# The last scan of a hybrid backbone with its gate units and weight splits in another order, and two query rotations of Mixer B in later steps

## The chip, the cores and the metric

The kernel runs on one core of a Trainium2 chip. The metric is device time in microseconds (us); lower is better. A kernel is timed in several executions, of which the median counts. One execution more is recorded by the profiler: its span runs from the first instruction to the last, and its own time is that of the whole launch. Below, TensorE is the matmul engine (PE in rows; PEld is its weight load), VectorE is DVE, ScalarE is ACT, GpSimd is POOL and SyncE is SP.

## The reference

The model is a block of four layers over 256 latent and 256 context tokens with 1024 features, in float32. The layers' mixers are A, B, C, A. Each layer has a mixer and an MLP, each behind an RMS norm with shift, scale and gate from a conditioning vector.

- Mixer A is a bidirectional mLSTM in chunks of 128 tokens with 8 heads: `h = num / max(|den|, exp(-m))` for each direction, the two directions added, then for each head `h * rsqrt(mean(h*h) + eps) * head_g`, and `(sigmoid(o) * h) @ w_out`, where `o` is 1024 columns of the projection `x @ w_in`. In the last layer only the latent tokens have an output.
- Mixer B is attention with 16 query heads and 4 key heads of 64 features. Latent queries and keys are turned by a 2-D rotary embedding; context ones are not. Scores go through a softmax with a learned sink for each head.

## The kernel before

All matrix products of weights are done as three float32r products: a weight tile of 128x1024 is loaded (`w_dma`, on SP's queue), cast to a high part on ScalarE (`w_hi`, line 242), and the low part is the difference, on VectorE (`w_lo`, line 247), which then issues the load of the tile four places on. `w_half` does the cast at once and returns the difference as a function to be called later; `w_get(0)` takes the next tile and splits it only if that was not done. There are 4 raw tiles and 5 pairs of parts. A unit is 128 output columns: 8 chunks of 3 matmuls (lines 392 to 394), and half a unit is 4 chunks.

The order on every engine is the order of the code; nothing is rescheduled. Waits are set by a tracker: two instructions on different engines wait for each other where they touch the same data, or the same of the eight PSUM banks.

**The last scan** (`scan`, with `last` true) goes over four head pairs, pr = 0 to 3. The output gate's 8 units (m = 0 to 7) are worked in between, in halves, by the generator `fillers`: every `next(fill)` issues half a unit into bank 4 (even m in its first 256 columns, odd m in the others). The sigmoid of a unit has three steps. The exponential (line 975, ScalarE) is issued with the unit's second half; the clamp on VectorE with Ln and Exp on ScalarE (lines 977 to 979) with the next unit's first half; the two combining operations on VectorE (lines 981 and 982) where `settle` is called. In an iteration stand:

- `states(pr)`: products of keys and values into columns 0 to 448 of banks 6 and 7 (line 1062), then six VectorE operations that read them (lines 1071 and 1073);
- a half unit; `mask` (VectorE, line 948) and `weights` (ScalarE, line 956) for the next pair; `outputs` (lines 1087 and 1096, banks 0 to 3);
- `out(pr - 1, hh)`: two transposes (line 1148) into columns 256 to 511 of bank 7 or 6, and line 1150 on VectorE that reads them and multiplies the gate;
- `keys` (line 1034, bank 5), `scores` (line 1026, columns 0 to 255 of banks 6 and 7), `keys_weigh` (line 1044) and `weigh` (line 1052, which reads the scores);
- the second half of the unit; `finish` (denominators on VectorE, then lines 1115 and 1117); `head_squares` (ScalarE); another unit's two halves; `head_norm` (three ScalarE and three VectorE operations on 128x4, then line 1140 on ScalarE).

Before the change the second unit's first half comes ahead of `head_norm` and its second half after it, each behind one `w_half`.

**Mixer B** projects ten units of queries and keys. `rotate` copies a unit's latent half to SBUF (line 1325), and its returned function `rest` does the rotation: a matmul with a permutation (line 1329), three VectorE operations (lines 1331 to 1333), and `put`: two copies on ScalarE (line 1317) and two subtractions on VectorE (line 1319). The functions wait in the list `pend`. The attention goes in steps y, two head pairs each: scores of the pairs 2y and 2y+1 (`s1`), their maxima on VectorE, exponentials on ScalarE, normalisation (`normalise(y - 1)`), transposes of the probabilities (`turn`) and, two steps on, value products (`pv`, line 1467). Pairs alternate between banks 3, 4 and banks 6, 7 for their scores. The unit 8 is projected ahead of step 1, the unit 9 at the end of step 1 in bank 2. Bank 2 is next used by the value products of step 5. The rotated queries of units 8 and 9 are first read in step 9.

Of the kernel before, what the change touches and what calls it, by code (L numbers as in the profile page):

```python
# [208 lines left out]
class Body:  # L209
# [748 lines left out]
    def scan(self, l, i, last, sp, lp, dnm, dar, qT, kT, vx, tok, saved, n):  # L958
# [6 lines left out]
        bk = self.banks  # L965
# [19 lines left out]
        def fillers():  # L985
            late = None
            for m in range(8):
                w = self.w_get(0)
                o = bk[4][:, m % 2 * T : m % 2 * T + T] if last else bk[4]
                self.unit(o, w, self.x_chunk, full, range(4))  # L990
                if late:
                    next(late)
                yield
                self.unit(o, w, self.x_chunk, full, range(4, NK))
                cur["late"] = late
                late = cur["last"] = sigmoid(m, o)
                next(late)
                yield
# [15 lines left out]
        def mask(pr, d):  # L1014
            self.scan_mask(pr, d)

        def weights(pr, d):
            self.scan_exp(pr, d, tok, outc)
# [11 lines left out]
        def keys(pr):  # L1030

            kt = bk[5].rearrange("p (c k) -> p c k", c=4)
            for tcn in range(4):
                nc.tensor.transpose(kt[:, tcn, :], kT[:, pr, tcn * 128 : tcn * 128 + 128], self.ident)
# [14 lines left out]
        def weigh(pr, d):  # L1049
            for hh in range(2):  # L1050
                e = cur["D", pr, d, hh]
                nc.vector.tensor_tensor(out=e, in0=e, in1=bk[6 + hh][:, :n], op=ALU.mult)
# [25 lines left out]
        def outputs(pr, sid):  # L1078


            def place(d, hh, c):
                return bk[2 * d + hh][:, (c % 2) * 256 : (c % 2) * 256 + 129]

            for d in range(2):
                for hh in range(2):
                    for c in (2 * sid, 2 * sid + 1):
                        nc.tensor.matmul(  # L1087
                            place(d, hh, c), lhsT=cur["D", pr, d, hh][:, c * 128 : c * 128 + 128], rhs=vx[:, c, 2 * pr + hh, :],
                            start=(c == 2 * sid), stop=False, skip_group_check=True,
                        )  # L1090
            for pos in (1,) if sid else (2, 3):
                for d in range(2):
                    c = ORDERS[d][pos]
                    for hh in range(2):
                        b = 64 * hh
                        nc.tensor.matmul(
                            place(d, hh, c), lhsT=cur["qa", pr, d][b : b + 64, c * 128 : c * 128 + 128],
                            rhs=cur["C", pr, d, pos - 1][b : b + 64, :], start=False, stop=True, skip_group_check=True,
                        )
# [44 lines left out]
        def out(pr, hh, tp=bk[5]):  # L1144
            h = 2 * pr + hh
            for c in range(nch):
                t_ = slice(c * 128, c * 128 + 128)
                nc.tensor.transpose(tp[:, t_], cur["h", pr, hh][:, t_], self.ident)
            hg = self.hgn[:, i * 8 + h : i * 8 + h + 1]
            nc.vector.scalar_tensor_tensor(  # L1150
                out=sg[:, h, :n], in0=tp[:, :n], scalar=hg, in1=sg[:, h, :n], op0=ALU.mult, op1=ALU.mult
            )

        fill = fillers()
# [7 lines left out]
        for d in range(2):  # L1162
            weigh(0, d)
        low = self.w_half()
        next(fill)
        for pr in range(4):
            more = pr < 3
            for hh in range(2):
                cur["h", pr, hh] = sp.tile([128, n], F32, tag="hacc", name="hacc", bufs=4)
            if more and not last:  # L1170
                self.scan_load(lp, pr + 1, dnm, dar, n, last)
            if more:
                self.scan_qa(lp, pr + 1, qT, n)
            if pr < 2 and last:
                self.scan_load(lp, pr + 2, dnm, dar, n, last)
            states(pr)
            if not last:
                outputs(pr, 1)
            if pr and not last:
                head_norm(pr - 1)  # L1180
            next(fill)
            if last:

                if pr:
                    out(pr - 1, 0, bk[7][:, 256:512])
                if more:
                    for d in range(2):
                        mask(pr + 1, d)
                        weights(pr + 1, d)
                outputs(pr, 0)  # L1190
                if more:
                    keys(pr + 1)
                    scores(pr + 1)
                    keys_weigh(pr + 1)
                    weigh(pr + 1, 0)
                    weigh(pr + 1, 1)
                next(fill)
                if not more:
                    split(0)
                    split(1)  # L1200
                finish(pr, 0)
                if pr:
                    out(pr - 1, 1, bk[6][:, 256:512])
                settle()
                low()
                if more:
                    head_squares(pr)
                    low = self.w_half()
                    next(fill)
                    head_norm(pr)  # L1210
                    low()
                    low = self.w_half()
                    next(fill)
                    settle()
                continue
            finish(pr, 1)
            if pr:
                out(pr - 1, 0)
            if more:
                mask(pr + 1, 0)  # L1220
            low()
            next(fill)
            if more:
                weights(pr + 1, 0)
                low = self.w_half()
            if pr:
                out(pr - 1, 1, bk[6])
            if more:
                mask(pr + 1, 1)
            settle()  # L1230
            if more:
                keys(pr + 1)
                weights(pr + 1, 1)
                next(fill)
                scores(pr + 1)
                keys_weigh(pr + 1)
            else:
                split(0)
                split(1)
            outputs(pr, 0)  # L1240
            if more:
                weigh(pr + 1, 0)
                weigh(pr + 1, 1)
                low()
                low = self.w_half()
                finish(pr, 0)
                head_squares(pr)
                next(fill)
                settle()
# [35 lines left out]
    def mixer_b(self, l, i):  # L1285
        nc, tc = self.nc, self.tc
        with ExitStack() as st:
# [5 lines left out]
            pend = []  # L1293
# [70 lines left out]
            bk = self.banks  # L1364
# [123 lines left out]
            def query(u, o, between, ahead):  # L1488
                w = self.w_get(ahead)
                self.unit(o, w, self.x_chunk, ALL, range(4))  # L1490
                between()
                self.unit(o, w, self.x_chunk, ALL, range(4, NK))
                evac(u, o, ALL)
# [17 lines left out]
            for y in range(1, N + 3):  # L1511
                more = y < N
                late = block_end(y - 4) if y >= 5 and y % 2 == 1 else None
                t = 2 * (y - 2)
                turns = 2 <= y < N + 2
                if more:
                    s1(2 * y)
                    maxima(2 * y)
                if y >= 3:
                    pv(y - 3)  # L1520
                if turns:
                    turn(t)
                if y == 2:
                    pend.pop(0)(bk[5])
                if y in (N, N + 1):
                    begin(bk[3 + 3 * (y - N)])
                if more:
                    exps(2 * y)
                    s1(2 * y + 1)
                    maxima(2 * y + 1)  # L1530
                if turns:
                    turn(t + 1)
                if late:
                    late()
                if more:
                    exps(2 * y + 1)
                if y <= N:
                    normalise(y - 1)
                if y in (N, N + 1):
                    begin(bk[4 + 3 * (y - N)])  # L1540
                if y == 1:
                    query(9, bk[2], lambda: pend.pop(0)(bk[5]), 0)
                if N - 3 <= y <= N + 1:
                    self.wsplit_to(self.wsplit + 1)
                if y > N:
                    c = slice(4 * (y - N - 1), 4 * (y - N - 1) + 4)
                    nc.gpsimd.dma_start(out=self.h[:, c, :], in_=saved[:, c, :])
# [336 lines left out]
```

## Time and profile before

| | us |
|---|---|
| time, median of 3 executions | 2101.82 |
| lowest, highest | 2101.45, 2102.55 |
| the profiled execution: its own time | 2103.67 |
| its span | 2101.8 |

| engine | share of the span busy |
|---|---|
| TensorE | 97% |
| TensorE weight load | 82% |
| VectorE | 70% |
| ScalarE | 45% |
| GpSimd | 4% |

A busy TensorE is one that has matmuls under way; it may still run at the lower of its two clocks. The granted clock of a stretch is 1.00 for 2.4 GHz and 0.50 for 1.2 GHz, and a mean of both in between. The last scan lies at about 1802 to 1886 us of the span, the attention of Mixer B at about 686 to 800.

### The profile page before, as it was taken

What the parts mean: (1) busy time and instruction counts of PE and PEld (TensorE: products, weight loads), DVE (VectorE), ACT (ScalarE), POOL (GpSimd) and SP (SyncE); (2) the same over time, 40 slices, a digit from 0 to 9 for tenths busy, and PEclk for the clock granted to TensorE, in tenths of its full rate; (3) what the DMA queues carried; (4) which work ended last, traced back from release to release, by engine and by line L of the source; (5) the groups of instructions that cost most, each with busy time, mean ns of one, the idle gap of its engine ahead of it and who ended that gap; (6) DMA issues with size and microseconds to landing.
All of it is one profiled execution on the core that took longest, in us unless ns stands there. A gap on an engine that the chain in (4) does not pass through costs nothing.

```text
span 2101.8 us, 29107 instructions
## 1 busy us (share of the span) xinstructions
PE 2038.5 (97%) x11154; PEld 1724.8 (82%) x11154; DVE 1472.1 (70%) x2600; ACT 943.6 (45%) x1778; POOL 81.5 (4%) x136
## 2 busy tenths in 40 slices
PE   6999999999999999999999999999999999979998
PEld 3778898888888768888888988888888898878997
DVE  5558768778778785777777754577777764567665
ACT  3437662423336674523324432362332445456554
POOL 0133000000000000000000000000000001200000
PEclk9999999999999999999999999999999999989999
DMA  9873437666653004455566233245656525436663
GB/s 298 276 232 111 136 96 207 188 194 198 186 154 130 2 26 146 143 179 190 183 189 190 81 120 99 81 148 178 188 185 189 175 87 158 115 95 191 184 187 92
DMA packets 96732, 326.03 MB, mean 155 GB/s; under 512 B 17728, under 2 KB 18896, under 8 KB 95696
## 3 DMA queue, kind: packets, MB, share of 16 engines
q1 hardware_dynamic: 81184, 293.81, 44.9%
q0 software_dynamic: 14864, 29.83, 4.7%
q8 instruction: 87, 1.43, 0.3%
q10 hardware_dynamic: 544, 0.52, 0.1%
q14 instruction: 53, 0.43, 0.1%
HBM read 319.73 MB, written 4.33 MB: 154 GB/s over the span
## 4 chain that ended last, share of the span: by engine, by line
PE 58%; DVE 2%; ACT 1%; issue 0%; DVEq 0%; ACTq 0%
PE bank L392 16%; PE bank L393 15%; PE bank L394 15%; PE bank L409 3%; PE bank L410 1%; PE bank L626 1%; PE bank L629 1%; PE bank L627 1%; PE bank L442 1%; PE bank L444 1%; PE bank L443 1%; PE bank L1087 0%; DVE wlo L247 0%; ACT whi L242 0%; DVE hacc L1117 0%
## 5 line engine op out<-in xcount | busy, mean ns | idle before, releaser
L392 PE MATMUL bank<-x,whi 128*128 128x512 f32 (+1 forms) x1568 | 570.5, 364 | 16.7 <-ACT h L975 13.9
L242 ACT CAST whi<-raw 128x1024 fp32r<-128x1024 f32 x374 | 388.0, 1046 | 416.9 <-PE bank L393 347.0
L247 DVE TENSOR_TENSOR wlo<-raw,whi 128x1024 fp32r<-128x1024 f32 x374 | 456.2, 1227 | 159.1 <-ACT whi L242 158.7
L393 PE MATMUL bank<-x,whi 128*128 128x512 f32 (+1 forms) x1568 | 564.9, 360 | 0.7 <-DVE x L1008 0.6
L394 PE MATMUL bank<-x,wlo 128*128 128x512 f32 (+1 forms) x1568 | 564.9, 360 | 0.0
L354 DVE SCALAR_TENSOR_TENSOR junk<-ada,cbc 128x1024 bf16<-128x1024 f32 x320 | 390.6, 1221 | 10.0 <-DMA ada<-in_ada 5.6
L392 PEld LDWEIGHTS bank<-x,whi 128*128 128x128 f32 x1568 | 298.9, 191 | 66.5 <-ACT h L975 16.3
L393 PEld LDWEIGHTS bank<-x,whi 128*128 128x128 f32 x1568 | 299.1, 191 | 44.1 <-DVE x L1008 1.2
L394 PEld LDWEIGHTS bank<-x,wlo 128*128 128x128 f32 x1568 | 299.0, 191 | 43.8
L392 PE MATMUL bank<-hh,whi 128*128 128x512 f32 (+1 forms) x872 | 321.1, 368 | 0.0
L393 PE MATMUL bank<-hh,whi 128*128 128x512 f32 (+1 forms) x872 | 320.5, 368 | 0.0
L394 PE MATMUL bank<-hh,wlo 128*128 128x512 f32 (+1 forms) x872 | 320.5, 368 | 0.0
L712 DVE TENSOR_TENSOR hh<-q,hh 128x512 fp32r<-128x512 f32 (+1 forms) x137 | 81.5, 595 | 161.7 <-ACT q L711 161.3
L709 ACT ACTIVATE r<-bank 128x512 f32<-128x512 f32 (+1 forms) x137 | 71.0, 518 | 267.0 <-PE bank L394 265.6
L392 PEld LDWEIGHTS bank<-hh,whi 128*128 128x128 f32 x872 | 164.4, 188 | 27.7
L393 PEld LDWEIGHTS bank<-hh,whi 128*128 128x128 f32 x872 | 164.4, 188 | 27.3
L394 PEld LDWEIGHTS bank<-hh,wlo 128*128 128x128 f32 x872 | 164.4, 188 | 27.0
L585 DVE SCALAR_TENSOR_TENSOR h<-bank,mod,h 128x256 f32<-128x256 f32 x248 | 110.1, 479 | 100.6 <-PE bank L394 100.6
L479 ACT ACTIVATE sq<-h 128x256 f32<-128x256 f32 (+1 forms) x74 | 36.2, 489 | 134.6 <-DVE h L585 114.2
L626 PE MATMUL bank<-x,whi 128*128 128x256 f32 x312 | 80.5, 287 | 3.5 <-ACT x L547 3.5
L409 PE MATMUL bank<-hh,whi 128*128 128x512 f32 x224 | 79.3, 399 | 0.0
L627 PE MATMUL bank<-x,wlo 128*128 128x256 f32 x312 | 79.3, 283 | 0.0
(281 smaller groups left out, 2381.3 us busy)
## 6 DMA issues: line engine op xcount, KB each, us to landing
raw<-in_wts SPq DMA_DIRECT2D x374, 512.0 KB, 4.0
ada<-in_ada SPq DMA_DIRECT2D x160, 512.0 KB, 3.7
start<-in_ada SPq DMA_DIRECT2D x16, 512.0 KB, 8.9
first<-in_ada POOLq DMA_DIRECT2D x12, 512.0 KB, 6.0
cbc<-line POOLq DMA_DIRECT2D x4, 1024.0 KB, 7.6
rb<-dnm POOLq DMA_DIRECT2D x16, 256.0 KB, 6.8
ab<-dar POOLq DMA_DIRECT2D x16, 256.0 KB, 10.0
h<-in_hin SPq DMA_DIRECT2D x4, 512.0 KB, 8.1
```

Of the source, the lines that this page charges most:

```text
L242: self.nc.scalar.copy(hi, self.raw[j])
L247: self.nc.vector.tensor_tensor(out=lo, in0=self.raw.pop(j), in1=hi.bitcast(F32), op=ALU.subtract)
L354: nc.vector.scalar_tensor_tensor(out=junk, in0=w, scalar=1.0, in1=self.cbc[:, s, :], op0=ALU.mult, op1=ALU.mult, accum_out=self.mods[l][:, ...
L392: mm(out, lhsT=whi, rhs=xhi, start=first, stop=False)
L393: mm(out, lhsT=whi, rhs=xlo, start=False, stop=False)
L394: mm(out, lhsT=wlo, rhs=xhi, start=False, stop=last)
L409: mm(o, lhsT=w[0][:, c], rhs=x2[:, :, LT], start=(k == 0), stop=(k == NK - 1))
L585: self.nc.vector.scalar_tensor_tensor(out=self.h[:, m, a:b], in0=o[:, a - sl.start : b - sl.start], scalar=mod[:, gate + m, s : s + 1], in ...
L626: mm(o[:, :T], lhsT=w[0][:, c], rhs=hi[:, sl], start=(k == 0), stop=False)
L627: mm(o[:, :T], lhsT=w[1][:, c], rhs=hi[:, sl], start=False, stop=False)
L709: nc.scalar.activation(r[:, :n], o, AF.Relu)
L712: nc.vector.tensor_tensor(out=hl[:, sl], in0=q[:, :n], in1=hh[:, sl].bitcast(F32), op=ALU.subtract)
```

## The change

In the last scan, both halves of the second unit are issued together, ahead of `head_norm`, so that the unit's exponential stands ahead of the norm in ScalarE's queue. The two casts of an iteration come together after `head_norm`, and their differences (`low`) are called in the next iteration: one ahead of `mask`, one behind `weights`. `out(pr - 1, 0)` moves from ahead of `mask` to behind `outputs`. In Mixer B the rotation of unit 8 moves from the middle of unit 9's projection to the end of step 2, the rotation of unit 9 from the middle of step 2 to the end of step 3, and both use bank 2 for the permutation, not bank 5.

```diff
--- before.py
+++ after.py
@@ -1162,6 +1162,7 @@
         for d in range(2):
             weigh(0, d)
         low = self.w_half()
+        lows = [low]
         next(fill)
         for pr in range(4):
             more = pr < 3
@@ -1181,13 +1182,16 @@
             next(fill)
             if last:
 
-                if pr:
-                    out(pr - 1, 0, bk[7][:, 256:512])
+                lows.pop(0)()
                 if more:
                     for d in range(2):
                         mask(pr + 1, d)
                         weights(pr + 1, d)
+                if lows:
+                    lows.pop(0)()
                 outputs(pr, 0)
+                if pr:
+                    out(pr - 1, 0, bk[7][:, 256:512])
                 if more:
                     keys(pr + 1)
                     scores(pr + 1)
@@ -1202,15 +1206,12 @@
                 if pr:
                     out(pr - 1, 1, bk[6][:, 256:512])
                 settle()
-                low()
                 if more:
                     head_squares(pr)
-                    low = self.w_half()
+                    next(fill)
                     next(fill)
                     head_norm(pr)
-                    low()
-                    low = self.w_half()
-                    next(fill)
+                    lows = [self.w_half(), self.w_half()]
                     settle()
                 continue
             finish(pr, 1)
@@ -1520,8 +1521,6 @@
                     pv(y - 3)
                 if turns:
                     turn(t)
-                if y == 2:
-                    pend.pop(0)(bk[5])
                 if y in (N, N + 1):
                     begin(bk[3 + 3 * (y - N)])
                 if more:
@@ -1539,7 +1538,9 @@
                 if y in (N, N + 1):
                     begin(bk[4 + 3 * (y - N)])
                 if y == 1:
-                    query(9, bk[2], lambda: pend.pop(0)(bk[5]), 0)
+                    query(9, bk[2], lambda: None, 0)
+                if y in (2, 3):
+                    pend.pop(0)(bk[2])
                 if N - 3 <= y <= N + 1:
                     self.wsplit_to(self.wsplit + 1)
                 if y > N:
```

## Rows read from the trace of the kernel before

**Rows 1.** The page's first part: busy time and share of the span, by engine.

```profile
PE 2038.5 (97%) x11154; PEld 1724.8 (82%) x11154; DVE 1472.1 (70%) x2600; ACT 943.6 (45%) x1778; POOL 81.5 (4%) x136
```

**Rows 2.** TensorE's waits, 1800 to 1900 us: waiter, releaser, us in total, times, longest.

```profile
PE bank L392 <- ACT h L975: 13.7, 4, 4.5
```

**Rows 3.** Timeline of TensorE, last scan: start, us, line, operation [idle before].

```profile
1815.15 0.39 PE L392 MATMUL bank<-x,whi 128*128 128x256 f32 x1 [0.47 <-ACT h L975]
...
1818.22 1.54 PE L1062 MATMUL bank<-vx,kw 128*64 128x129 f32 x24
1824.27 0.58 PE L392 MATMUL bank<-x,whi 128*128 128x256 f32 x1 [4.51 <-ACT h L975]
...
1834.52 0.44 PE L1148 MATMUL bank<-cons,hacc 128*128 128x128 f32 x2
...
1838.07 1.54 PE L1062 MATMUL bank<-vx,kw 128*64 128x129 f32 x24
...
1868.37 1.16 PE L1096 MATMUL bank<-C,ab 64*128 64x129 f32 x16
```

**Rows 4.** Stretches: busy us (instructions) of PE, PEld, DVE, ACT, POOL, clock, DMA.

```profile
1824.27:1827.00 2.73, 2.73 (x12) 2.73 (x13) 1.00 (x5) 0.84 (x2) 1.27 (x3) 0.50 0.62 207
...
1847.07:1856.50 9.43, 9.37 (x85) 8.29 (x83) 7.04 (x22) 5.58 (x22) 0.00 (x0) 1.00 0.01 3
...
1838.07:1856.50 18.43, 14.02 (x122) 12.70 (x121) 12.39 (x37) 10.84 (x36) 1.83 (x4) 0.91 0.25 75
```

**Rows 5.** Timeline of ScalarE, last scan.

```profile
1823.84 0.38 ACT L975 ACTIVATE h<-bank 128x256 f32<-128x256 f32 x1
...
1871.19 0.39 ACT L975 ACTIVATE h<-bank 128x256 f32<-128x256 f32 x1 [6.91 <-PE bank L394]
```

**Rows 6.** Timeline of VectorE, last scan.

```profile
1816.92 0.42 DVE L981 SCALAR_TENSOR_TENSOR h<-h,ssum 128x256 f32<-128x256 f32 x1
...
1847.27 0.48 DVE L1150 SCALAR_TENSOR_TENSOR h<-bank,hgn,h 128x256 f32<-128x256 f32 x1 [2.32 <-PE bank L1148]
1847.67 1.42 DVE L948 TENSOR_TENSOR rb<-rb,cons 128x256 f32<-128x256 f32 x4
1850.74 1.16 DVE L1044 TENSOR_TENSOR kw<-bank,tok 128x512 f32<-128x512 f32 x2 [1.65 <-PE bank L1034]
...
1855.60 0.42 DVE L981 SCALAR_TENSOR_TENSOR h<-h,ssum 128x256 f32<-128x256 f32 x1
...
1856.40 1.22 DVE L247 TENSOR_TENSOR wlo<-raw,whi 128x1024 fp32r<-128x1024 f32 x1
1857.53 0.28 DVE L977 TENSOR_SCALAR h<-h 128x256 f32<-128x256 f32 x1
1859.17 0.16 DVE L514 TENSOR_TENSOR ha<-hy 128x4 f32<-128x4 f32 x1 [1.36 <-ACT hy L510]
...
1859.72 1.22 DVE L247 TENSOR_TENSOR wlo<-raw,whi 128x1024 fp32r<-128x1024 f32 x1
...
1861.65 0.48 DVE L1071 COPY C<-bank 128x129 f32<-128x129 f32 x2
...
1863.09 0.29 DVE L977 TENSOR_SCALAR h<-h 128x256 f32<-128x256 f32 x1
```

**Rows 7.** Timeline of TensorE, Mixer B.

```profile
711.87 0.39 PE L1383 MATMUL bank<-K,Q 128*128 128x256 f32 x1 [2.65 <-ACT p L1419]
...
712.81 3.81 PE L1467 MATMUL bank<-h,vv 128*64 128x256 f32 x16
...
720.39 1.95 PE L1467 MATMUL bank<-h,vv 128*64 128x256 f32 x16
```

**Rows 8.** Timeline of ScalarE, Mixer B.

```profile
710.38 0.85 ACT L1317 ACTIVATE Q<-t 64x256 fp32r<-64x256 f32 x2 [1.87 <-DVE t L1333]
```

**Rows 9.** Timeline of VectorE, Mixer B.

```profile
709.13 0.42 DVE L1331 TENSOR_TENSOR t<-bank,cons 128x256 f32<-128x256 f32 x1
...
710.82 0.87 DVE L1319 SCALAR_TENSOR_TENSOR Q<-t,Q 64x256 fp32r<-64x256 f32 x2 [0.48 <-ACT Q L1317]
```

## The prediction

> **What bounds the kernel now.** The page comes first: TensorE is busy for 97% of the span [rows 1], so a change of a microsecond has to remove a TensorE wait, a low clock, or work of TensorE. The change removes no work, so I listed TensorE's waits in the last scan. Between 1800 and 1900 us nearly all the waiting has one cause: line 392, the first matmul of a half gate unit, waits 13.7 us in four times for the exponential of line 975 [rows 2]. The timeline of TensorE shows where. The first wait, of 0.47 us, is in the iteration pr = 0; the first of the long ones, 4.51 us, stands right behind the state products of pr = 1 [rows 3]. The other two long ones stand at the same place in pr = 2 and 3; (13.7 - 0.47 - 4.51) / 2 gives 4.4 each. What follows a long wait runs at the lower clock: the twelve matmuls of the half unit take 2.73 us at a granted clock of 0.50, which is 1.2 GHz; without that they would take half, 1.37 [rows 4]. The iteration from 1838.07 to 1856.50 has 14.02 us of TensorE, 12.39 of VectorE and 10.84 of ScalarE work in 18.43 us [rows 4]: with the hole gone, VectorE is close behind.
>
> **Why line 975 is late.** The even half unit and the odd one share bank 4, in two halves of its columns, and the new unit waits until the old one's exponential has been read, though it writes other columns: the wait of 0.47 us is such a case [rows 3]. In the code of before, ScalarE's queue holds the whole head norm and a weight cast between the unit's first half and that exponential; so it starts at 1823.84 [rows 5], though its products were done before the state products began at 1818.22 [rows 3].
>
> **The scan after the change.** The number of instructions is the same; the order changes. ScalarE's queue now reads: squares, Ln and Exp of the unit before, the exponential, then head norm, then both casts. VectorE's reads, from the add-multiply of line 1150 for the first head: line 1150, keys, weighing, denominators, line 1117, line 1150 for the second head, two combining operations, clamp, norm, two combining operations, six states, clamp, split, four masks, split. I walk this queue, for it is now the longest, by start to start in the rows [rows 6]: line 1150 0.40 (1847.27 to 1847.67); keys up to the combining 4.86 (1850.74 to 1855.60, the wait for line 1115 included); combining 0.80 (to 1856.40); clamp up to the norm 1.64 (1857.53 to 1859.17; that is the time of Ln, Exp and the norm's two activations), plus 0.4 for the exponential that now stands among them [rows 5]; norm 0.55 (to 1859.72); combining 0.80 again; states 1.44 (1861.65 to 1863.09); clamp 0.29; two splits of 1.13 (1856.40 to 1857.53); masks 1.42. The sum is 14.86 us for an iteration, against 19.85 for pr = 1 (1818.22 to 1838.07 [rows 3]) and 18.43 for pr = 2 [rows 4].
>
> The start is the combining operation of pr = 0 at 1816.92 [rows 6]; the split behind it is gone. From there: 0.80 + 2.04 + 0.55 + 0.80 + 1.44 + 0.29 + 1.13 + 1.42 + 1.13 = 9.60, so line 1150 of pr = 1 comes at 1826.52, of pr = 2 at 1841.38. Up to the end of the states of pr = 3 it is 0.40 + 4.86 + 0.80 + 2.04 + 0.55 + 0.80 + 1.44 = 10.89 more: 1852.27. Then TensorE does what is left of pr = 3: line 1096 up to the unit's exponential takes 2.82 (1868.37 [rows 3] to 1871.19 [rows 5]), and the two transposes moved there 0.44 [rows 3]. The exponential would then come at 1855.5 where it was at 1871.19, and what follows (splits of x, denominators, output products) is the same chain as before. **Term one: -15.7 us.**
>
> TensorE fits under this: the next unit's first half waits for the exponential, which follows the clamp by Ln and Exp, about when the state products end, so some 0.1 to 0.3 us remain of the 4.4.
>
> **What is late next.** The transposes of the first head now come after the output products and just before keys and scores. They write columns 256 to 511 of bank 7; VectorE's line 1150 reads them; scores write columns 0 to 255 of bank 7. Line 1150 stands behind clamp, split, masks and split. From the end of the states it takes 0.29 + 1.13 + 1.42 + 1.13 + 0.48 = 4.45 to be done; TensorE has line 1096 (1.16), two transposes (0.44 [rows 3]) and the keys' four (at most 0.9) to do meanwhile, and then waits some 2 us at scores. Behind scores are the unit's second half and its exponential. This hole appears in pr = 1 and 2 (pr = 3 has no scores). It is on no path longer than the 14.86, because VectorE itself is the path, but it may cost clock. The trace of before has nothing between these instructions, but it has the like in bank 4, the wait of 0.47 us for a reader of other columns [rows 3]. The Trainium skill, PSUM — Partial Sum Buffer, section "PSUM bank collisions raise a hardware error", says that accesses are to be guarded by bank, not by address. By that rule scores wait in full; guarded by address they would not wait, VectorE's 14.86 would stay, and only the clock's price would go. The 0.47 us wait speaks for the rule.
>
> Clock: a hole of 4.5 us lowered it for at least one half unit, +1.36 us [rows 4]; one of 2.65 in Mixer B made sixteen matmuls take 3.81 instead of 1.95 [rows 7]. For two holes of 2 us I have both ends: nothing, or up to two half units at the low clock, 2.7 each. The second half at low clock delays the exponential, and the queue behind it on ScalarE, by about half of the 1.36. I take 0.6 each: **term two, +1.2 us.**
>
> The weight splits: each split also lets SP issue the load of a tile. The first issue now comes at the start of pr = 0's exponentials, not at its end, and the later ones no later than before against the units that read them. No unit reads a tile that is split less than two half units before it, so I take 0. In pr = 0 the split stands ahead of the masks, 1.13 us, under TensorE's output products: 0. POOL's queue keeps its order; its loads wait for line 1096 and come earlier.
>
> **Mixer B.** Before, the second rotation sits in step 2: VectorE's three operations from 709.13 and the two subtractions from 710.82 [rows 9] follow the first maxima, and ScalarE's two copies wait for VectorE 1.87 us, at 710.38 [rows 8]; the exponential of the step queues behind them. TensorE waits 2.65 us for it at 711.87, and the value products then run at the low clock, 3.81 instead of 1.95 [rows 7]. The most to gain is 2.65 + 1.86 = 4.5. The two rotations carry 710.82 + 0.87 - 709.13 = 2.56 us of VectorE each, now at the ends of steps 2 and 3, ahead of the next maxima. Were all that TensorE's, 5.1 would come back: 0.6 slower. Step 2's first exponential comes 2.1 us earlier (at 709.13, where its maxima are done, not at 710.38 + 0.85), so most of the hole and its low clock go. The rotations come back in two places: the transposes of step 3 wait for copies that stand behind the first rotation's, and the scores of step 5 for exponentials behind the second. The value products of a step, 1.95 us [rows 7], cover between half and all of themselves of each 2.56, which leaves 1.6 or 0.6; I take 1.1 each. **Term three: -4.5 + 2.2 = -2.3 us.**
>
> **Sum.** -15.7 + 1.2 - 2.3 = -16.8 us. The profiled execution took 2103.67 us (span 2101.8 and 1.87 around it), which becomes 2086.9; its median of three runs is 1.85 lower, 2101.82, which becomes 2085.0. After the scan nothing is reordered and TensorE goes on as the bound, so all of it shifts by the same amount.
>
> **Rivals.**
> - *No clock is lost* in the scan, and Mixer B gives all: 15.7 + 4.5 = 20.2, 2081.6. For it: holes half as long as those that show the low clock. Against: VectorE does gain 5.1 us of work in two steps.
> - *The holes at scores lower the clock for two half units each*, and Mixer B gives nothing: 15.7 - 5.4 = 10.3, 2091.5. For it: 2.65 us was enough in Mixer B [rows 7].
> - *The exponential stays late*, because another of its waits takes over, and only Mixer B counts: 2099.5, no change. Against: nothing but clamp, Ln and Exp stands ahead of it.
> - *The low clock never leaves the scan*: the place is the hole at scores, once an iteration, and TensorE then stays at 1.2 GHz until the next. Its 14.02 us contain 1.36 of low clock already, so 12.7 at full clock become 25.3 us at half, with 2 of the hole 27.3; two iterations take 54.6 instead of 38.3, 16.3 more; pr = 0 and 3 stay as they are, Mixer B gives 2.3: 2115.8. It decides from the point where an iteration takes over 19.1 + 1.2 us (half of the 2.3 allowed for). Against: after the hole of pr = 2 the clock is back at 1.00 from 1847.07 to 1856.50 [rows 4]. The Trainium skill, TensorE: Matmul & The Clock Gate, "What's actually happening", calls the low clock the default state that activity releases; by that alone repeated holes would give this rival. The same row speaks against it here.
>
> **How the numbers follow.** Forecast 0.60 (its own range 2082 to 2089), the first rival 0.15, the second 0.18, no change 0.04, slower 0.03. A measurement of this kernel tells 0.2%, about 4.2 us, from no change. The first three are all faster: 0.93. The range 2080 to 2092 holds them but for their tails.
>
> **What would show it.** Right: after the state products of pr = 1 to 3 line 392 waits under 0.5 us; the state products of pr = 1, 2 and 3 stand about 15 us apart; a new wait of TensorE of about 2 us at line 1026 (scores) in pr = 1 and 2, released by line 1150; in Mixer B the 2.65 us are gone, and smaller waits stand two and three steps on. Wrong: line 392 still waiting for line 975 for over 2 us, an iteration above 17 us, a granted clock of 0.5 through most of one, or a unit that waits for its split (line 247).

## The result, and the profile after

The changed kernel takes 2087.38 us, median of six executions (2086.52 to 2089.88); the kernel before takes 2101.93 beside it (2101.45 to 2102.98). The ratio is 0.9932 with a 95% interval of 0.9919 to 0.9945: 14.5 us or 0.7% faster. The forecast was 2085.0, 16.8 us faster. The profiled execution has a span of 2088.1 us and a time of 2089.88, the longest of the six.

TensorE's waits in the last scan, from the waits of the changed kernel (waiter, releaser, us in total, times, longest):

```profile
PE bank L1026 <- DVE h L1150: 3.7, 2, 1.9
PE bank L392 <- DVE h L1150: 1.9, 1, 1.9
...
PE bank L392 <- ACT h L975: 0.7, 2, 0.5
```

The 13.7 us for line 975 [rows 2] are down to 0.7 us. A new wait of 3.7 us in two times has come at scores (line 1026), released by line 1150. The wait of 1.9 us of line 392 for line 1150 stands after the scan's loop; it was there before (1.95 us).

The timeline of TensorE in the changed kernel (start, us, line, operation, idle before), to be read beside [rows 3]:

```profile
1818.19 1.54 PE L1062 MATMUL bank<-vx,kw 128*64 128x129 f32 x24
...
1827.27 0.71 PE L1026 MATMUL bank<-qT,kT 64*128 64x128 f32 x6 [1.80 <-DVE h L1150]
...
1833.13 1.54 PE L1062 MATMUL bank<-vx,kw 128*64 128x129 f32 x24
...
1842.35 0.71 PE L1026 MATMUL bank<-qT,kT 64*128 64x128 f32 x6 [1.95 <-DVE h L1150]
...
1849.45 1.54 PE L1062 MATMUL bank<-vx,kw 128*64 128x129 f32 x24
...
1861.33 0.58 PE L392 MATMUL bank<-x,whi 128*128 128x256 f32 x1 [1.95 <-DVE h L1150]
```

The state products of pr = 1 stand at 1818.19, before at 1818.22: up to here the two executions have gained nothing on one another. Those of pr = 2 stand 14.94 us later (19.85 before), those of pr = 3 16.32 after them (18.43 before). In both iterations scores wait 1.8 to 1.95 us. The chain of VectorE, beside [rows 6], and of ScalarE, beside [rows 5], in the changed kernel:

```profile
1823.72 1.96 DVE L948 TENSOR_TENSOR rb<-rb,cons 128x256 f32<-128x256 f32 x4
...
1826.74 0.47 DVE L1150 SCALAR_TENSOR_TENSOR h<-bank,hgn,h 128x256 f32<-128x256 f32 x1
...
1838.80 1.96 DVE L948 TENSOR_TENSOR rb<-rb,cons 128x256 f32<-128x256 f32 x4
1840.69 1.21 DVE L247 TENSOR_TENSOR wlo<-raw,whi 128x1024 fp32r<-128x1024 f32 x1
1841.83 0.47 DVE L1150 SCALAR_TENSOR_TENSOR h<-bank,hgn,h 128x256 f32<-128x256 f32 x1
```

```profile
1833.87 0.37 ACT L975 ACTIVATE h<-bank 128x256 f32<-128x256 f32 x1
1834.13 0.29 ACT L509 ACTIVATE ha<-ss,eps 128x4 f32<-128x4 f32 x1
...
1857.34 0.38 ACT L975 ACTIVATE h<-bank 128x256 f32<-128x256 f32 x1 [2.35 <-PE bank L394]
```

From line 1150 of pr = 1 at 1826.74 to that of pr = 2 at 1841.83 it is 15.09 us; the walk gave 14.86, and 1826.52 for the first. The unit's exponential at 1833.87 stands ahead of the norm (1834.13). The last one comes at 1857.34, before at 1871.19.

The stretches of the two iterations in the changed kernel (length, busy us of PE, PEld, DVE, ACT, POOL, clock, DMA share, GB/s), and of the part behind the hole of pr = 2:

```profile
1818.19:1833.13 14.94, 12.88 (x121) 11.62 (x120) 12.75 (x36) 10.66 (x36) 6.12 (x10) 1.00 0.47 140
1833.13:1849.45 16.32, 14.33 (x121) 12.90 (x120) 12.75 (x36) 11.49 (x37) 2.10 (x4) 0.90 0.28 88
1842.35:1848.90 6.55, 6.50 (x41) 5.98 (x42) 5.26 (x17) 3.03 (x15) 0.00 (x0) 0.74 0.29 81
```

The iteration of pr = 1 keeps the clock at 1.00 in spite of its hole; that of pr = 2 does not. Behind its hole the mean is 0.74, and TensorE's busy time is 14.33 where it is 12.88 in the other. That is 1.45 us for one low clock.

Mixer B of the changed kernel, TensorE, beside [rows 7] (line numbers are one higher there):

```profile
709.73 2.04 PE L1468 MATMUL bank<-h,vv 128*64 128x256 f32 x16
...
714.44 1.15 PE L1447 MATMUL bank<-cons,p 128*128 128x128 f32 x8 [1.18 <-ACT h L1451]
...
722.77 0.50 PE L1384 MATMUL bank<-K,Q 128*128 128x512 f32 x1 [1.73 <-ACT p L1420]
...
724.23 1.85 PE L1468 MATMUL bank<-h,vv 128*64 128x256 f32 x8
...
735.18 2.02 PE L1468 MATMUL bank<-h,vv 128*64 128x256 f32 x16
```

and the same place at the end in the kernel before:

```profile
735.16 2.02 PE L1467 MATMUL bank<-h,vv 128*64 128x256 f32 x16
```

The value products of step 3 run at full clock now, 2.04 us, and start at 709.73, 3.1 us earlier than before. Then the transposes wait 1.18 us and the scores of step 5 wait 1.73 us, and the products behind these run at the low clock, 1.85 us where 1.08 is usual. A third wait, of 0.85 us, follows at the transposes of step 6. At 735.18 the kernel is where it was at 735.16. In this execution Mixer B gained and gave back.

### The profile page after: what moved, and what is told of

Same layout as the page of the kernel before. It is cut to its first block, busy times and chain, and to the rows that moved or that the text cites. A ratio compares the mean times of both kernels' runs of the same rounds, so it can differ in the third digit from the quotient of the medians.

```text
span 2088.1 us, 29108 instructions
## 1 busy us (share of the span) xinstructions
PE 2033.4 (97%) x11154; PEld 1721.3 (82%) x11154; DVE 1474.5 (71%) x2600; ACT 941.6 (45%) x1778; POOL 83.4 (4%) x136
## 3 DMA queue, kind: packets, MB, share of 16 engines
q8 instruction: 87, 1.43, 0.3%
```

## The experiments

All were timed in five rounds beside the kernel before. The parts alone, the exponential alone and scores first ran on one chip; the split in the gap and the kernels with one rotation moved, with both edits and changed again on a second; casts and splits alone and transposes early on a third.

**The parts alone.** The first kernel has the scan as changed and the two hunks of Mixer B undone; the second has these two hunks alone:

```diff
-                if y == 2:
-                    pend.pop(0)(bk[5])
...
-                    query(9, bk[2], lambda: pend.pop(0)(bk[5]), 0)
+                    query(9, bk[2], lambda: None, 0)
+                if y in (2, 3):
+                    pend.pop(0)(bk[2])
```

> The scan as changed, Mixer B as before. Theory A (read from the two traces: at the state products of pr = 1 of the last scan both stand at the same time, 1818.22 and 1818.19 us, so Mixer B brought nothing): the whole gain is the scan's, 13.5 to 15.5 us against the kernel before. Theory B (the forecast's third term, 2.3 us, is real and hidden by a later start of the profiled run): only 12 to 12.5 us.

> The two rotations as changed, the scan as before. Theory A: within 0.7 us of the kernel before; the wait of 2.65 us goes and three smaller ones (1.2, 1.7 and 0.9 us) with a low clock after the second take its place. Theory B: 2.3 us faster.

Measured: the scan alone 2087.24 against 2103.29, ratio 0.9924 (0.9912 to 0.9936), 16.0 us; Mixer B alone 2103.11, ratio 0.9997 (0.9988 to 1.0005). Theory A holds: the gain is the scan's (theory B's 12.5 lies outside its interval, 13.5 to 18.5 us; the 16.0 is a little over A's 15.5). Mixer B's part can't be told from nothing by these times, and not from the forecast's 2.3 us either, which its interval (2.5 faster to 1.1 slower) just holds; the traces say more, below. TensorE's waits of Mixer B in the second kernel:

```profile
PE bank L1383 <- ACT p L1419: 4.2, 8, 1.7
PE bank L1446 <- ACT h L1450: 1.2, 1, 1.2
...
PE bank L1446 <- DVE p L1434: 0.5, 1, 0.5
```

The wait of 2.65 us has become three, 1.7 (the longest of the first row), 1.2 and 0.5.

**The exponential alone.** The kernel before, with the two halves of the unit together:

```diff
                     low = self.w_half()
                     next(fill)
+                    next(fill)
                     head_norm(pr)
                     low()
                     low = self.w_half()
-                    next(fill)
                     settle()
```

> The kernel before with one edit: the second unit's two halves together, ahead of the head norm; casts, splits and the place of the first head's transposes as before. Theory A (VectorE's queue and bank 7 set the iteration): the wait for line 975 falls to about 1 us, but the transposes then wait some 3 us for the states that are read out of bank 7, as VectorE comes to these only after two splits; an iteration of 16 to 17 us, 5 to 8 us faster than before. Theory C (the late exponential was all there was): 13 us or more faster, and the moved splits and transposes are worth nothing.

Measured: 2098.88, ratio 0.9985 (0.9976 to 0.9993), 4.4 us, a little under the 5 to 8 of theory A and far from theory C. Its state products stand 17.98 and 18.17 us apart, where A said 16 to 17. TensorE's waits in its last scan:

```profile
PE bank L1148 <- DVE C L1073: 8.6, 3, 2.9
PE bank L392 <- ACT h L975: 3.0, 4, 1.0
```

The long waits for line 975 are gone, but the transposes now wait 8.6 us in three times for VectorE to read the states out of bank 7. The hole of 4.4 us has moved by a few instructions and kept 2.9 us of itself.

**The casts and splits alone.** The kernel before, with both casts after the second half and their differences called around masks and weights:

```diff
...
+                lows.pop(0)()
                 if more:
                     for d in range(2):
                         mask(pr + 1, d)
                         weights(pr + 1, d)
+                if lows:
+                    lows.pop(0)()
                 outputs(pr, 0)
...
-                low()
                 if more:
                     head_squares(pr)
-                    low = self.w_half()
                     next(fill)
                     head_norm(pr)
-                    low()
-                    low = self.w_half()
                     next(fill)
+                    lows = [self.w_half(), self.w_half()]
                     settle()
```

> The kernel before with the casts and splits moved as in the change, nothing else: the second unit's halves stand on either side of the head norm, the transposes where they were. Theory A: the exponential is no longer behind a split on VectorE (1.13 us) and a cast on ScalarE (0.94 us), so the three long waits for line 975 shrink from 4.4 to about 2.3 us, and the splits run where VectorE waited for TensorE: 6 to 8 us faster than before. Theory C (the exponential's place alone matters): the waits stay at about 4 us, within 2 us of before.

Measured: 2094.10 against 2101.47, ratio 0.9969 (0.9958 to 0.9979), 7.4 us. TensorE's waits for the exponential in its last scan:

```profile
PE bank L392 <- ACT h L975: 7.4, 4, 2.3
```

The longest is 2.3 us, as worked out, though the exponential still stands behind the norm. So the splits are the larger part: 7.4 us alone against 4.4 for the exponential alone. The intervals of the two (4.4 to 8.8 and 1.5 to 5.0 us, on different chips) overlap, but the traces agree: from the state products of pr = 1 to those of pr = 3 it is 38.28 us before, 36.15 with the exponential alone and 33.25 with the splits alone. The two add to 11.8; with both and the transposes where they were (transposes early, below) it is 12.8, and with the transposes moved as well 14 to 16. What the move of the transposes adds is within the spread.

**Is TensorE's hole at scores the path?** Two kernels take it away and leave the amount of VectorE's work as it is. The first issues keys and scores ahead of the transposes (its edit is shown), the second puts the first head's transposes back ahead of the split and the masks:

```diff
                 outputs(pr, 0)
+                if more:
+                    keys(pr + 1)
+                    scores(pr + 1)
                 if pr:
                     out(pr - 1, 0, bk[7][:, 256:512])
                 if more:
-                    keys(pr + 1)
-                    scores(pr + 1)
                     keys_weigh(pr + 1)
```

> The changed kernel with keys and scores issued ahead of the first head's transposes, so that scores no longer wait for line 1150; VectorE's queue is the same. Theory A (VectorE's queue is the path, the hole of TensorE at scores a symptom): the two waits of 1.8 and 1.95 us go, the iterations stay at 14.5 to 15 us, and at most the low clock behind the second hole comes back: 0 to 1.5 us faster than the changed kernel, 14.5 to 16 us faster than before. Theory D (the hole is the path): each iteration loses its hole, 3.7 us more, 18 us faster than before.

> The changed kernel with the first head's transposes back in front of the split and the masks; the casts, splits and the two halves together stay as changed. Theory A (VectorE's queue is the path): the hole at scores goes, a wait of about 1.2 us at the transposes for the states takes its place, iterations stay at 14.5 to 16 us, and the time is within 2 us of the changed kernel (13 to 17 us faster than before). Theory G (the move of the transposes is what makes the change work): it loses half of the gain, 7 us faster than before.

Measured: scores first 2086.63 against 2103.29, ratio 0.9921 (0.9909 to 0.9933), 16.7 us, the same as the scan alone on that chip; transposes early 2088.70 against 2101.47, ratio 0.9941 (0.9929 to 0.9954), 12.8 us, just below theory A's figure. TensorE's waits in the last scan, scores first:

```profile
PE bank L1148 <- DVE rb L1052: 4.7, 2, 2.6
...
PE bank L392 <- ACT h L975: 0.5, 1, 0.5
```

and transposes early:

```profile
PE bank L1148 <- ACT whi L242: 5.2, 3, 1.7
...
PE bank L1148 <- DVE rb L1052: 1.9, 2, 1.1
```

In the first, nothing waits at scores, but the second head's transposes now wait 4.7 us for line 1052, which reads the scores on VectorE. In the second, the first head's transposes wait 1.7 us each time, and the second's again for line 1052. The releaser of the 1.7 us is printed as a cast of ScalarE; the transposes read nothing of it, and what they need comes at that time from the states on VectorE (these end at 1820.72, the transposes start at 1820.87). Take a hole away and it opens where TensorE next needs VectorE. Theory G's 7 us lies outside the interval of the second kernel, 9.7 to 14.9. Theory D's 18 lies inside that of the first, 14.1 to 19.1, so times alone don't reject it; its iterations do. They are 16.40 and 15.74 us, where D takes 1.8 and 1.95 off the 14.94 and 16.32 of the changed kernel. They are above theory A's 14.5 to 15 as well: two holes of 2.6 and 2.1 us both lowered the clock (0.90 in each iteration). With transposes early, at full clock, they are 15.09 and 15.63. So far the hole looks like a symptom; that VectorE's queue is the path is tested next.

**Is it VectorE's length, then?** One split moves into the stretch where VectorE waits for the norm's activations:

```diff
-                if lows:
+                if lows and not more:
                     lows.pop(0)()
                 outputs(pr, 0)
...
                     next(fill)
                     next(fill)
+                    if lows:
+                        lows.pop(0)()
                     head_norm(pr)
```

> The changed kernel with the second split of an iteration moved from behind the masks to VectorE's idle time of 1.6 to 2.0 us ahead of the head norm (in the last pair it stays). Theory A (VectorE's queue sets the iteration): each of the two full iterations gets shorter by one split, 1.1 us, and the hole at scores shrinks from 1.9 to about 0.8 us, which ends the low clock behind it: 2 to 4.5 us faster than the changed kernel on the same chip. Theory E (the queue has no such slack, since ScalarE's chain of Ln, Exp, exponential and norm sets the end): within 1 us of the changed kernel.

Measured: 2086.09 against 2103.06, ratio 0.9918 (0.9904 to 0.9931), 2.7 us below the changed kernel on that chip (2088.83). The timeline of VectorE in it:

```profile
1824.31 0.47 DVE L1150 SCALAR_TENSOR_TENSOR h<-bank,hgn,h 128x256 f32<-128x256 f32 x1
...
1830.54 1.22 DVE L247 TENSOR_TENSOR wlo<-raw,whi 128x1024 fp32r<-128x1024 f32 x1
1832.25 0.16 DVE L514 TENSOR_TENSOR ha<-hy 128x4 f32<-128x4 f32 x1 [0.49 <-ACT hy L510]
...
1836.37 1.42 DVE L948 TENSOR_TENSOR rb<-rb,cons 128x256 f32<-128x256 f32 x4
1837.71 0.48 DVE L1150 SCALAR_TENSOR_TENSOR h<-bank,hgn,h 128x256 f32<-128x256 f32 x1
```

The split stands where 1.62 us were idle; 0.49 are left before the norm. Its iterations are 14.33 and 13.41 us long (state products at 1816.37, 1830.70 and 1844.11). By the size of the gain this is theory A; theory E's 1 us is not excluded by times that spread over 4 us, but the iterations rule it out. The queue accounts for them: from line 1150 of pr = 1 to that of pr = 2 it is 13.40 us here, and the changed kernel's 15.09 less the split's 1.13, less the 0.54 by which the masks are shorter here (1.42, not 1.96; the reason is in the last section), is 13.42.

**Mixer B with one rotation moved.** Unit 8's rotation goes back into the middle of unit 9's projection, and unit 9's comes at the end of step 2:

```diff
-                    query(9, bk[2], lambda: None, 0)
-                if y in (2, 3):
+                    query(9, bk[2], lambda: pend.pop(0)(bk[5]), 0)
+                if y == 2:
                     pend.pop(0)(bk[2])
```

> The changed kernel with unit 8's rotation back in the middle of unit 9's projection; only unit 9's goes to the end of step 2, in bank 2. Theory A (each late rotation costs Mixer B what its 2.6 us of VectorE take from the steps' slack, and two in a row lowered the clock): one wait of about 1.2 us at the transposes of step 3 remains, the wait of 1.7 us at the scores of step 5 and the low clock behind it go: 2 to 3.5 us faster than the changed kernel. Theory F (the steps have no slack, what goes in comes out): within 1 us.

> Both edits of the two kernels above. Theory A: their gains add, 4 to 8 us faster than the changed kernel, about 20 us faster than before. If E and F hold: no faster.

> The changed kernel itself, for the comparison on this chip: 14 to 17 us faster than before. Every theory expects the same; the place of the low clock in the scan should differ from the first profile, as it did in the scan alone.

Measured on the same chip: one rotation late 2088.66, ratio 0.9932 (0.9920 to 0.9945), by its time no better than the changed kernel again, 2088.83, ratio 0.9931 (0.9919 to 0.9944), 14.2 us as expected; both edits 2082.30, ratio 0.9902 (0.9888 to 0.9915). The waits of Mixer B with one rotation late are smaller:

```profile
PE bank L1384 <- ACT p L1420: 2.8, 8, 1.0
PE bank L1447 <- ACT h L1451: 1.9, 2, 1.2
```

From the scores of step 1 to the value products of step 7 it takes 35.56 us (696.62 to 732.18), in the changed kernel 36.15 or 37.73 by the execution, before 37.93. So its profile is 0.6 to 2.2 us better, and its times don't show it: executions of one kernel differ by 2 to 4 us here. The expectation of 2 to 3.5 us was a miss as far as the times go. Both edits together are the fastest version, 6.5 us below the changed kernel and 20.8 below the kernel before; that is more than the two gains add to by the times. In the profiled executions of the two kernels, 4.7 us apart, 4.1 lie between the state products of pr = 1 and pr = 3 (28.27 against 32.40) and 0.6 in Mixer B (35.55 against 36.15); the rest, 1.4 us earlier ahead of Mixer B and as much later behind the scan, is in stretches where no instruction differs. What the medians show beyond 4.7 I can't place. Its two iterations, at full clock, and its line 1150 of pr = 1 and 2 with the masks between them:

```profile
1813.46:1827.79 14.33, 12.89 (x122) 11.63 (x121) 12.21 (x36) 10.57 (x36) 5.64 (x10) 1.00 0.42 108
1827.79:1841.73 13.94, 12.87 (x122) 11.61 (x121) 12.73 (x37) 10.80 (x36) 3.00 (x4) 1.00 0.30 101
```

```profile
1821.39 0.47 DVE L1150 SCALAR_TENSOR_TENSOR h<-bank,hgn,h 128x256 f32<-128x256 f32 x1
...
1833.46 1.96 DVE L948 TENSOR_TENSOR rb<-rb,cons 128x256 f32<-128x256 f32 x4
1835.34 0.47 DVE L1150 SCALAR_TENSOR_TENSOR h<-bank,hgn,h 128x256 f32<-128x256 f32 x1
```

14.33 and 13.94 us, of which TensorE works 12.9. From line 1150 to line 1150 it is 13.95 us, again the changed kernel's 15.09 less the split's 1.13; the masks take 1.96 in both. With this the queue of VectorE is shown to be the path. In the changed kernel again the clock fell behind the hole of pr = 2, as in the first profile (1.00 and 0.90 in iterations of 15.51 and 16.89 us), so the expectation that the place would differ failed.

## Why the prediction was right, point by point

- *What bounds the scan* was right. The late exponential and the order of VectorE's queue were the cause; the walked queue gave 14.86 us for an iteration and 1826.52 for its start, and the trace shows 15.09 and 1826.74. Behind the state products line 392 doesn't wait for the exponential at all; under 0.5 us was said.
- *The 0.2 us of difference in the walk* are two errors of opposite sign. The four masks take 1.89 us from their start to the next (1838.80 to 1840.69), where I put 1.42, and the two clamps with the added exponential together take about 0.2 less than I put. GpSimd's product (line 941) now falls beside the masks, from the timeline of GpSimd in the changed kernel:

```profile
1823.93 0.80 POOL L941 TENSOR_TENSOR ab<-ab,qT 128x256 f32<-128x256 f32 x1
...
1839.01 0.80 POOL L941 TENSOR_TENSOR ab<-ab,qT 128x256 f32<-128x256 f32 x1
```

- *What is late next* was right in place, size and harmlessness: scores wait for line 1150, 1.80 and 1.95 us, and moving that wait elsewhere gained nothing.
- *Term two*, the clock, was 1.2 us for two holes. One hole lowered it, for 1.45 us, the other did not; the place differs by execution (in the scan alone it was the hole of pr = 1).
- *Term one* with term two was 14.5 us up to the last exponential; measured 1871.19 - 1857.34, less the 0.03 of the start, is 13.8.
- *Between the last exponential and the end of the scan's own output products* I had called the chain the same. It was 1.4 us shorter: before, the low clock lasted from 1875.19 to 1881.2, 6.0 us, and now from 1861.33 to about 1864.5. That was luck of the clock.
- *After the scan*, "all of it shifts by the same amount" failed by 1.5 us in the profiled execution. From the first matmul of line 409, behind the scan's own output products, to the end it is 215.44 us before and 216.98 after, with not one instruction moved. Behind a wait of 3.5 us for the norm of the last MLP the clock fell in this execution; in another execution of the same kernel it did not, and there the stretch took 215.42. Of the twelve profiled executions three took 215.4 to 215.5 and nine 216.9 to 217.8; the two with the scan of before are among the three, so whether it is chance alone stays open. The changed kernel, and its second profile:

```profile
1891.47 0.39 PE L626 MATMUL bank<-x,whi 128*128 128x256 f32 x1 [3.53 <-ACT x L547]
```
```profile
1889.00:1895.00 6.00, 3.53 (x17) 3.53 (x18) 5.64 (x15) 2.95 (x7) 0.00 (x0) 0.73 0.34 96
```

```profile
1890.03 0.39 PE L626 MATMUL bank<-x,whi 128*128 128x256 f32 x1 [3.53 <-ACT x L547]
```
```profile
1887.60:1893.60 6.00, 3.57 (x30) 3.57 (x31) 5.64 (x15) 2.95 (x7) 0.00 (x0) 1.00 0.32 90
```

- *Term three*, Mixer B, is the term of the sum that was mis-sized: -2.3 us, measured 0.6 alone by the ratio (from 2.5 faster to 1.1 slower), and 0.2 in the stretch up to 735.18. The second rival, by which Mixer B gives nothing, was nearer here. The 4.5 us did go and the two waits did come where the walk put them (transposes of step 3, scores of step 5), at 1.18 and 1.73 us against 1.1 each. What I had left out is that the second can lower the clock in its turn: the products behind it then take 1.85 instead of 1.08, and the next transposes and scores are slow too. Six profiled executions have both rotations late. In three of them that low clock came, and the stretch from the scores of step 1 to the value products of step 7 took 37.71 to 37.73 us; in three it did not, and it took 36.13 to 36.15. With Mixer B as before it took 37.18 to 37.93 in four, 37.63 in the mean. So the term was worth nothing or 1.5 us, by the execution.

In the profiled executions 16.8 became 13.8: less 2.3 for Mixer B, less 0.7 up to the last exponential, less 1.5 for the clock that fell after the scan, and 1.4 more for the one that rose sooner in it. The median's 14.5 is nearer, since the profiled execution is the longest of its six. That the total is off by only 3.0 us there owes something to luck: misses of 4.5 us one way and 1.4 the other.

## What to carry to other kernels

When a wait is removed, walk the queue of the engine that set it, from start to start in the rows, and find its length: the new time is that queue, whatever holes the other engine then shows. Try a hole by moving it before working on it; if it reopens at the next place where the two engines meet, look instead for idle time in the queue that is the path, and put work there. Check each new wait of TensorE for whether it costs clock.

## What the runs showed of the hardware

- TensorE's clock does not answer alike to the same wait. The wait of 1.73 us at the scores of step 5 lowered it in three executions (the value products behind it took 1.85 to 1.98 us) and not in three others (1.08); holes of 1.80 to 1.95 us in the scan did in some and not in others, and one of 3.5 us did and did not in the same kernel (0.73 and 1.00 above). The falls read here cost 1.4 to 1.6 us each, and the one of 6.0 us behind the last exponential of the kernel before about twice that; executions of one kernel differ by 2 to 4 us. The Trainium skill, TensorE: Matmul & The Clock Gate, section "What's actually happening", says that the number of slow matmuls at the start of one kernel varies from run to run; the granted clock of 20 to 30 us of the span, 0.73 and 0.66 in two executions of the changed kernel, agrees with it, and the falls show the like later on.
- Four operations of VectorE that read two SBUF tensors (line 948) take 1.42 or 1.43 us alone and 1.95 to 1.97 with a product of GpSimd (line 941) beside them, without exception between 1790 and 1850 us of the twelve traces. DMA issues of GpSimd beside them cost nothing (1.42 at 1820.05 with both edits). That VectorE waits out the whole product is seen in the kernel before, where an operation that takes 0.16 us elsewhere started with the product and ended with it:

```profile
1820.49 0.72 POOL L941 TENSOR_TENSOR ab<-ab,qT 128x256 f32<-128x256 f32 x1
1820.50 0.73 DVE L514 TENSOR_TENSOR ha<-hy 128x4 f32<-128x4 f32 x1 [1.36 <-ACT hy L510]
```

Beside the next product, at 1823.75, the operations of line 1073, which read one SBUF tensor, a column of factors and PSUM, kept their 1.13 us. The Trainium skill, SBUF — State Buffer, section "Who interferes with whom", says that the two engines share a port pair as an exclusive lock, and that a VectorE instruction with two SBUF inputs contends with a GpSimd instruction that reads SBUF; the traces agree.
